# Threshold attention on one core: GpSimd made to wait for two-operand DVE steps, and a new order of all steps

## The chip, the cores and the metric

The kernel runs on one core of one Trainium2 chip. The metric is the device time of one execution in microseconds (us). The kernel before took 198.44 us (median of 3 runs, 197.9 to 199.52).

## The reference

Inputs are Q, K and V with 8 batches, 12 heads, 512 positions and 64 dimensions in float32, and a threshold of 0.1.

```
scores  = einsum('bhqd,bhkd->bhqk', Q, K) / sqrt(64)
weights = exp(scores - max(scores))
weights = weights / (sum(weights) + 1e-10)
weights = where(weights > 0.1, weights, 0)
weights = weights / (sum(weights) + 1e-10)
out     = einsum('bhqk,bhkd->bhqd', weights, V)
```

A row of weights has 512 entries with sum 1. With these inputs hardly any weight passes 0.1, so nearly every row of the output is zero.

## The kernel before, in words

The kernel writes zeros to the whole output and then computes only the few rows in which some weight may pass the threshold. There are 96 heads, taken as 48 pairs (two heads, one on each half of the partitions) and as 24 quads (two pairs, one load of K and Q).

**First part, all rows, in 16 bits.** For each quad SP (SyncE) issues the loads of K (L357) and Q (L361). TensorE transposes K (L392), ACT or DVE copies it from PSUM as float32 (L400, L402), GpSimd casts it to float16 (L411). GpSimd casts Q to float16 (L382), TensorE transposes it (L421), DVE copies it from PSUM (L427). For each pair there are four score steps (`sc`, L449, two matmuls each). Each score matmul fills one PSUM bank, and one exponent step (`ex`) empties it: on ACT with its exponential (L458) or on DVE with an integer approximation (L460). There are 384 exponent steps. The sum step (`sm`, L479, four matmuls) adds the exponents and a sharpened copy of them into a sum bank in PSUM, which collects a group of pairs. The groups have 24, 22 and 2 pairs (the last with L495). There is one sum bank.

**End of a group.** When all its sums are in, `y` (L521 on ACT), `d` (L532), `fl` (L537) and `mx` (L541) on DVE find the rows that may hold a large weight; `d` reads the sum bank for the last time, after which the next group's sums may begin.

**Second part, the rows found, in float32.** A group is followed by stages of up to 8 pairs (7 stages in all: three for group 0, three for group 1, one for group 2). A stage x runs `m` (L550, DVE), `ix` (L556, PE), `qi` (L561, DVE: the row numbers), `gq` (L567, GpSimd: an indirect DMA gathers the rows of Q), `xm` (L575 or L578, PE), `xev` (L585 or L587), `xqk` (L600 or L594, PE: scores against the float32 K that was kept), `xexp` (L606, ACT), `xcut` (L610), `xkeep` (L614), `oi` (L625) and `vi` (L619) on DVE, `gv` (L629, GpSimd: gathers rows of V) and `scatter` (L641, GpSimd: writes them to the output).

**Norms, a check on the 16-bit part.** For each quad `bits` squares the float16 Q and K: on GpSimd as two products (L436), on ACT (L438), or on DVE as a shift (L440). `norms` (L510, PE, four matmuls) adds the squares, and `nm` (L528, DVE) takes their maximum. For quads 0 to 7 the norms lie in spare rows of the sum banks of groups 0 and 1, and `nm` reads those banks at the end of the group; for quads 8 to 23 they have a PSUM bank of their own at the end. The checks (L789 to L804) end in one matmul (L813) and a branch: if a check fails, a slow exact loop runs.

**Order.** All steps of all engines stand in one table, `ORDER` (L13): a word is a step's number and its engine. Each engine runs its steps in that order, and an instruction waits only for the data and buffers that it needs. DVE and GpSimd stand in no fixed order to each other, except through such data. Buffers come from pools: 7 PSUM banks called `one`, 32 large SBUF buffers called `big` (loads, transposed K, float16 pairs, squares). `warm` steps (L367) run matmuls on zeros at the start, `spare` steps (L371, 20 of two matmuls each) run idle matmuls near the end; in the table of before they stand between the last norms.

Of the kernel before, what the change touches and what calls it, by code (L numbers as in the profile page):

```python
# [94 lines left out]
def kernel(  # L95
# [130 lines left out]
    is_norm = consts.tile([P, len(NORMS)], f32)  # L226
# [177 lines left out]
    def do_kh(eng, q, n):  # L404
        dst, src = qk_b[big("qk", q)][:, 1, n, :], kt_b[big("kt", q)][:, n, :]
        if eng == "ACT":
            nc.scalar.copy(dst, src)
        elif eng == "DVE":
            nc.vector.tensor_copy(dst, src)
        else:  # L410
            nc.gpsimd.tensor_copy(dst, src)  # L411
# [483 lines left out]
```

## Time and profile before

| what | value |
|---|---|
| runs | 199.52, 197.9, 198.44 us (median 198.44) |
| profiled execution | 198.32 us, its span 196.1 us, mean granted TensorE clock 0.945 |
| PE busy | 171.2 us (87%) |
| DVE busy | 164.8 us (84%), 369 instructions |
| ACT busy | 147.0 us (75%), 294 instructions |
| GpSimd (POOL) busy | 139.2 us (71%), 212 instructions |
| data moved | 38.28 MB, 195 GB/s over the span |

The span is from the first to the last instruction; the time of an execution holds 2.2 us more. A busy share is a mean over stages with different limits. A DVE instruction that has started and is held up counts as busy, so DVE's share contains such waits. A granted clock of 1.00 is 2.4 GHz and of 0.50 is 1.2 GHz; a value between is a mean over a stretch that holds both.

### The profile page before, as it was taken

Reading aid. Unit: us, or ns where it says so; the run is one execution under the profiler, and the core shown is the slowest. Engines: PE = TensorE matmul, PEld = TensorE weight load, DVE = VectorE, ACT = ScalarE, POOL = GpSimd, SP = SyncE. Lnnn points to the kernel's source line nnn. Section 1 sums busy time; section 2 is a strip of 40 time slices with the busy share of each in tenths; the row PEclk is TensorE's granted clock in tenths of the full one; section 3 lists DMA queues with packets and bytes.
Section 4 is the critical chain, followed back from the end, with each engine's and each line's share of the span. In section 5 each row is a group of like instructions: output and inputs, shape, how many; then the busy total and the mean of one; then the engine's idle time right before and its main releaser. Section 6 shows DMA issues by size and latency. Waiting matters only on the chain. (4 is left out here: it accounts for less than half of the span.)

```text
span 196.1 us, 6072 instructions
## 1 busy us (share of the span) xinstructions
PE 171.2 (87%) x2312; PEld 71.5 (36%) x2312; DVE 164.8 (84%) x369; ACT 147.0 (75%) x294; POOL 139.2 (71%) x212
## 2 busy tenths in 40 slices
PE   5799999999999997799799799999298396999960
PEld 2344343443443342243342343334032134643540
DVE  7769999999999997789999999999969957579320
ACT  0879999999999997989799699989169129483100
POOL 5459889999795999089999984969729441515570
PEclk9999999999999999999999999999859667599998
DMA  6998998998998979799879853699990000000000
GB/s 152 280 256 194 276 259 228 292 217 199 282 230 272 295 240 313 270 333 241 315 209 323 220 160 76 133 283 410 415 388 15 0 5 1 5 3 3 6 6 4
DMA packets 67550, 38.28 MB, mean 195 GB/s; under 512 B 52035, under 2 KB 64446, under 8 KB 67520
## 3 DMA queue, kind: packets, MB, share of 16 engines
q1 hardware_dynamic: 64464, 36.97, 67.5%
q10 hardware_dynamic: 2384, 0.79, 1.7%
q8 instruction: 18, 0.29, 0.6%
q0 software_dynamic: 672, 0.13, 0.5%
q14 instruction: 12, 0.10, 0.2%
HBM read 25.58 MB, written 12.79 MB: 196 GB/s over the span
## 5 line engine op out<-in xcount | busy, mean ns | idle before, releaser
L458 ACT ACTIVATE e<-one 128x512 f16<-128x512 f32 x228 | 118.6, 629 | 17.9 <-PE one L449 15.3
L460 DVE TENSOR_SCALAR e<-one 128x512 uint16<-128x512 f32 x156 | 99.5, 681 | 4.6 <-PE one L449 2.9
L449 PE MATMUL one<-big 64*128 64x512 f16 x384 | 71.9, 401 | 10.9 <-DVE e L460 7.3
L436 POOL TENSOR_TENSOR big<-big 128x512 bf16<-128x512 f16 x56 | 57.7, 1055 | 4.6 <-PE one L392 4.6
L479 PE MATMUL sum<-e,w_s 128*32 128x512 f16 x736 | 57.9, 403 | 0.4 <-DVE y L532 0.4
L411 POOL CAST big<-big 128x512 f16<-128x512 f32 x47 | 28.6, 624 | 9.6 <-ACT big L400 4.2
L449 PEld LDWEIGHTS <-big 64*128 64x128 f16 x384 | 18.9, 97 | 44.6 <-issue 37.9
L382 POOL CAST qh<-big 128x512 f16<-128x512 f32 x47 | 28.4, 619 | 8.7 <-DMA big<-in_Q_dram 7.1
L479 PEld LDWEIGHTS <-w_s 128*32 128x32 f16 x736 | 14.6, 98 | 31.9 <-issue 25.8
L400 ACT COPY big<-one 128x512 f32<-128x512 f32 (+1 forms) x38 | 20.9, 580 | 4.2 <-PE one L392 2.2
L427 DVE COPY big<-one 128x512 f16<-128x512 f16 (+1 forms) x52 | 19.6, 396 | 4.9 <-PE one L421 3.4
L392 PE MATMUL one<-identity_f,big 64*128 64x64 f32 x384 | 18.5, 236 | 2.8 <-DMA big<-in_K_dram 1.3
L392 PEld LDWEIGHTS one<-identity_f,big 64*128 64x128 f32 x384 | 16.8, 148 | 8.3 <-issue 1.8
L567 POOL DMA_INDIRECT qs<-in_Q_dram,idx x7 | 7.3, 1047 | 16.3 <-DVE idx L561 15.0
L629 POOL DMA_INDIRECT vr<-in_V_dram,idx x7 | 7.2, 1022 | 8.3 <-DVE idx L619 5.7
L440 DVE TENSOR_SCALAR big<-big 128x512 int32<-128x512 int32 x16 | 12.9, 838 | 0.1
L421 PEld LDWEIGHTS <-qh 64*128 64x128 f16 x384 | 8.9, 99 | 10.4 <-issue 5.0
L421 PE MATMUL one<-identity_h,qh 64*128 64x64 f16 x384 | 11.0, 197 | 1.8 <-POOL qh L382 1.0
L600 PE MATMUL one<-big,xq 128*32 128x512 f32 x92 | 10.9, 596 | 0.0
L402 DVE COPY big<-one 128x512 f32<-128x512 f32 (+1 forms) x14 | 9.0, 645 | 1.9 <-PE one L392 1.3
L641 POOL DMA_INDIRECT out_dram<-vr,idx x7 | 7.0, 1006 | 3.4 <-issue 3.3
L606 ACT ACTIVATE one<-one 128x512 f32<-128x512 f32 (+2 forms) x7 | 4.1, 579 | 6.7 <-PE one L600 4.2
(100 smaller groups left out, 108.1 us busy)
## 6 DMA issues: line engine op xcount, KB each, us to landing
out_dram<-zero SPq DMA_DIRECT2D x24, 512.0 KB, 6.8
big<-in_K_dram SPq DMA_DIRECT2D x92, 128.0 KB, 4.7
big<-in_Q_dram SPq DMA_DIRECT2D x22, 512.0 KB, 4.8
big<-in_Q_dram SPq DMA_DIRECT2D x3, 256.0 KB
big<-in_K_dram ACTq DMA_DIRECT2D x4, 128.0 KB, 4.8
big<-in_Q_dram ACTq DMA_DIRECT2D x1, 256.0 KB
qs<-in_Q_dram,idx POOLq DMA_INDIRECT x7
vr<-in_V_dram,idx POOLq DMA_INDIRECT x7, 2.3
```

The source lines that it names most:

```text
L382: nc.gpsimd.tensor_copy(dst, src)
L392: nc.tensor.matmul(dst[i][:, c:c + D], lhsT=src[ps, n0 + n, r, :], rhs=identity_f32[ps, ps], is_transpose=True, start=True, stop=True)
L400: nc.scalar.copy(dst, src)
L411: nc.gpsimd.tensor_copy(dst, src)
L421: nc.tensor.matmul(dst[i][:, c:c + D], lhsT=src[ps, n0 + n, r, :], rhs=identity_h[ps, ps], is_transpose=True, start=True, stop=True)
L427: nc.vector.tensor_copy(qk_b[big("qk", q)][:, 0, n0:n0 + k, i * SO * D:(i + 1) * SO * D], src)
L436: nc.gpsimd.tensor_tensor(out=dst[:, n, :], in0=src[:, n, :], in1=src[:, n, :], op=ALU.mult)
L440: nc.vector.tensor_scalar(dst.rearrange("p n c -> p (n c)").bitcast(i32), src.rearrange("p n c -> p (n c)").bitcast(i32), 2, 0x1FFF1FFF, o ...
L449: nc.tensor.matmul(one[at("one", ("sc", hp, t, h))][:], lhsT=qk[ps, 1, n, t * P:(t + 1) * P], rhs=qk[ps, 0, n, :], start=True, stop=True)
L458: nc.scalar.activation(dst, src, ACTF.Exp, scale=scale, bias=-11.0 * math.log(2.0))
L460: nc.vector.tensor_scalar(dst.bitcast(u16), src, scale * LOG2E * 1024.0, 4096.0, op0=ALU.mult, op1=ALU.add)
L479: nc.tensor.matmul(dst[32 * j:32 * j + 32, :], lhsT=w, rhs=x, start=first, stop=False, skip_group_check=True)
```

## The change

GpSimd's casts and products get a wait. Each DVE step that reads two SBUF operands, or copies or shifts from SBUF to SBUF (`qcast`, `kh`, `bits`, `fl`, `m`), is noted by `alone`; the next cast or product of GpSimd in the table waits until that DVE step has ended (`behind`). GpSimd's indirect DMAs get no such wait. `oi` no longer reads two SBUF tensors: a new DVE step `qf` writes a float copy of the output index, and `oi` takes it as a scalar operand. The norms of quads 0 to 7 leave the sum banks and get a `one` bank for themselves, as those of quads 8 to 23 have; `nm` runs twice, not three times, and no longer stands between a group's sums and the release of the sum bank. `warm` has 8 steps, not 5. `ORDER` is another table.

```
-    WARM = 5
+    WARM = 8
+    last_pair = [None]
+    def alone(inst):
+        last_pair[0] = inst
+        return inst
+    def behind(inst):
+        if last_pair[0] is not None:
+            tc.add_manual_dep(inst.ins, last_pair[0].ins.name,
+                              mybir.DependencyInfo(mybir.DependencyClass.Sync, mybir.DependencyReason.DATA),
+                              reason="one engine at a time on the shared port")
+            last_pair[0] = None
+        return inst
 ...
-            nc.gpsimd.tensor_copy(dst, src)
+            behind(nc.gpsimd.tensor_copy(dst, src))
 ...
-                nc.gpsimd.tensor_tensor(out=dst[:, n, :], in0=src[:, n, :], in1=src[:, n, :], op=ALU.mult)
+                behind(nc.gpsimd.tensor_tensor(out=dst[:, n, :], in0=src[:, n, :], in1=src[:, n, :], op=ALU.mult))
 ...
-        if q < LATE:
-            g = norm_of[q]
-            assert g in begun
-            dst, i, first = sum_b[at("sum", g)], norm_of[:q].count(g), False
-        else:
-            dst, i, first = one[at("one", "late")], q - LATE, "late" not in begun
+        part = int(q >= LATE)
+        dst, i = one[at("one", ("norms", part))], q - PARTS[part][0]
 ...
-        nc.vector.scalar_tensor_tensor(out=idx_b[at("ix", x)][0:n, 0:2],
-                                       in0=one[at("one", ("ix", x))][0:n, 0:1].to_broadcast([n, 2]), scalar=-1.0,
-                                       in1=base[0:n, 0:2, x], op0=ALU.mult, op1=ALU.add)
+        nc.vector.tensor_scalar(idx_b[at("ix", x)][0:n, 0:1], one[at("one", ("ix", x))][0:n, 0:1], -1.0,
+                                base[0:n, 0, x:x + 1], op0=ALU.mult, op1=ALU.add)
+    def do_qf(eng, x):
+        nc.vector.tensor_scalar(ix_b[at("ix", x)][0:n, :], one[at("one", ("ix", x))][0:n, 0:1], -1.0,
+                                base[0:n, 1, x:x + 1], op0=ALU.mult, op1=ALU.add)
 ...
-        nc.vector.scalar_tensor_tensor(out=to, in0=accs[0:n, x:x + 1], scalar=-(FAR - S), in1=to, op0=ALU.max, op1=ALU.add)
+        nc.vector.tensor_scalar(idx_b[at("ix", x)][0:n, 2:3], accs[0:n, x:x + 1], -(FAR - S), ix_b[at("ix", x)][0:n, :],
+                                op0=ALU.max, op1=ALU.add)
```

Counted in the two tables: exponents on ACT 228, then 232; on DVE 156, then 152. `bits` on GpSimd 28 in both, on DVE 16, then 12, on ACT 4, then 8. Copies of K from PSUM on ACT 38, then 36, on DVE 14, then 16. `y` of groups 1 and 2 on ACT, then of group 1 on DVE and of group 2 on ACT. In the new table all of norms 0 to 7 stand together at the end of group 0, 16 norms stand together behind the last `xqk`, and the 20 `spare` steps stand last of all, behind the checks.

## Rows read from the trace of the kernel before

**Rows 1.** Busy time by stretch: PE, PEld, DVE, ACT, POOL, granted clock, DMA share, GB/s
```profile
8.00:14.00 6.00, 5.52 (x54) 2.24 (x51) 4.25 (x11) 4.52 (x11) 3.96 (x12) 1.00 1.21 249
...
20.00:138.00 118.00, 112.70 (x1647) 45.00 (x1640) 112.00 (x207) 110.78 (x223) 100.83 (x156) 1.00 0.93 255
138.00:147.00 9.00, 5.32 (x59) 2.03 (x58) 7.11 (x9) 3.01 (x7) 4.40 (x6) 0.63 1.00 404
...
151.40:160.60 9.20, 5.58 (x54) 1.88 (x56) 7.78 (x11) 2.51 (x5) 3.77 (x5) 0.64 0.01 2
160.60:171.00 10.40, 8.84 (x110) 5.00 (x106) 6.40 (x16) 6.54 (x13) 4.04 (x4) 0.66 0.02 4
```

**Rows 2.** Timeline of DVE: start, duration, line, tiles, count
```profile
91.55 1.70 DVE L440 TENSOR_SCALAR big<-big 128x512 int32<-128x512 int32 x2
...
108.10 1.96 DVE L625 SCALAR_TENSOR_TENSOR idx<-accs,idx 128x1 int32<-128x1 f32 x1
...
136.23 4.86 DVE L625 SCALAR_TENSOR_TENSOR idx<-accs,idx 128x1 int32<-128x1 f32 x1
...
149.12 5.26 DVE L440 TENSOR_SCALAR big<-big 128x512 int32<-128x512 int32 x1
```

**Rows 3.** Timeline of POOL in the same stretch, with its idle time in brackets
```profile
139.04 2.03 POOL L436 TENSOR_TENSOR big<-big 128x512 bf16<-128x512 f16 x2
145.67 2.04 POOL L436 TENSOR_TENSOR big<-big 128x512 bf16<-128x512 f16 x2 [4.60 <-PE one L392]
...
152.07 2.02 POOL L436 TENSOR_TENSOR big<-big 128x512 bf16<-128x512 f16 x2
```

**Rows 4.** Timeline of PE: its first matmul after the stall
```profile
141.74 1.63 PE L449 MATMUL one<-big 64*128 64x512 f16 x5 [3.66 <-DVE e L460]
```

**Rows 5.** One line's instructions: duration in ns, least, median and longest
```profile
L625 DVE SCALAR_TENSOR_TENSOR idx<-accs,idx x7: 157/198/4862, 108.1 to 184.8; 128x1 int32<-128x1 f32 x5, 96x1 int32<-96x1 f32 x1, 64x1 int32<-64x1 f32 x1
...
L440 DVE TENSOR_SCALAR big<-big x16: 408/424/5259, 18.9 to 177.5; 128x512 int32<-128x512 int32 x16
```

**Rows 6.** Exponents on ACT (L458) by stretch: busy time, clock, DMA
```profile
20.00:138.00 118.00, 94.89 (x184) 1.00 0.93 255
138.00:161.00 23.00, 8.40 (x17) 0.70 0.41 163
```

**Rows 7.** Exponents on DVE (L460) by stretch
```profile
20.00:138.00 118.00, 80.17 (x126) 1.00 0.93 255
138.00:161.00 23.00, 9.29 (x15) 0.70 0.41 163
```

**Rows 8.** Groups by line and shape: count, busy us, mean ns, idle before
```profile
L458 ACT ACTIVATE e<-one 128x512 f16<-128x512 f32 x228 | 118.6, 629 | 17.9 <-PE one L449 15.3 <-PE one L510 1.6 <-issue 0.4
L460 DVE TENSOR_SCALAR e<-one 128x512 uint16<-128x512 f32 x156 | 99.5, 681 | 4.6 <-PE one L449 2.9 <-PE one L510 1.3
...
L600 PE MATMUL one<-big,xq 128*32 128x512 f32 x92 | 10.9, 596 | 0.0
...
L438 ACT ACTIVATE big<-big 128x1024 bf16<-128x1024 f16 x4 | 4.3, 1072 | 0.0
...
L619 DVE TENSOR_SCALAR idx<-accs,base 128x1 int32<-128x1 f32 x5 | 1.0, 204 | 0.0
```

**Rows 9.** Timeline of all engines from the end of group 1 to the end
```profile
161.14 0.69 DVE L528 TENSOR_REDUCE nmax<-sum 128x1 f32<-128x512 f32 x1 [1.62 <-PE sum L479]
...
166.22 1.02 POOL L567 DMA_INDIRECT qs<-in_Q_dram,idx  x1 [4.36 <-DVE idx L561]
...
180.76 0.62 PE L510 MATMUL one<-big,w_n 128*32 128x512 bf16 x8
...
187.25 2.05 PE L371 MATMUL one<-identity_f 128*128 128x128 f32 x16
...
190.44 0.09 PEld L813 LDWEIGHTS one<-identity_f,okm 128*1 128x1 f32 x2 [1.33 <-DVE nmax L528]
```

**Rows 10.** DMA issues: KB each, median us from issue to landing
```profile
big<-in_Q_dram SPq DMA_DIRECT2D x22, 512.0 KB, 4.8
```

More of the change, by code (lines that the diff above doesn't have):

```diff
@@ L131 @@
     LATE = 8
-    NORMS = (4, 4)
-    norm_of = [g for g, k in enumerate(NORMS) for _ in range(k)]
-    assert sum(NORMS) == LATE and all(GROUPS[g] + 2 * k <= 32 for g, k in enumerate(NORMS)) and 2 * (NQ - LATE) <= 32
+    PARTS = (range(0, LATE), range(LATE, NQ))
+    assert all(2 * len(k) <= 32 for k in PARTS)
     J = 8
@@ L408, in do_kh @@
         elif eng == "DVE":
[L409 removed]
+            alone(nc.vector.tensor_copy(dst, src))
         else:
[L411 removed]
+            behind(nc.gpsimd.tensor_copy(dst, src))
     def do_qtr(eng, u):
@@ L730 @@
             gives=[("big", ("qk", q))])
[L731 to L734 removed]
+        part = int(q >= LATE)
+        head = PARTS[part][0]
+        after = [("norms", head)] if q > head else [("sc", NP - 3, 0)] if part else []
+        add(("norms", q), {"PE": 0.22}, 0.23, [("bits", q, 1)] + after, 8 * q + (9 if q < LATE else 60),
+            lambda e, q=q: do_norms(e, q), takes=[("one", ("norms", part))] if q == head else [], gives=[("big", ("v", q))], mode="c")
         add(("z", q), {"SP": 0.6}, 0.1, [("sc", 2 * q, 0), ("const", 0)], 8 * q - 6, lambda e, q=q: do_zero(e, q))
@@ L740 @@
             gives=[("one", "spare")] if j == SPARE - 1 else [], mode="c")
-    add(("nm", "late"), {"DVE": 0.6}, 0.12, [("norms", q) for q in range(LATE, NQ)], 9999, lambda e: do_nm(e, "late"),
-        gives=[("one", "late")])
+    for part, qs in enumerate(PARTS):
+        add(("nm", part), {"DVE": 0.6}, 0.12, [("norms", q) for q in qs], 9999 if part else 8 * LATE + 20,
+            lambda e, part=part: do_nm(e, part), gives=[("one", ("norms", part))])
     for g in range(NG):
@@ L751 @@
         sums = [("sm", hp, t) for hp in pairs for t in range(SO)]
-        norms = [("norms", q) for q in range(LATE) if norm_of[q] == g]
         step("y", {"DVE": 0.6, "ACT": 0.5}, 0.12, sums, do_y, takes=[("y", g)])
         step("d", {"DVE": 0.64}, 0.12, ["y"], do_d)
-        if norms:
-            step("nm", {"DVE": 0.6}, 0.12, sums + norms, do_nm, pr=pr + 3)
-        add(("sumdone", g), {"NONE": 0.0}, 0.0, [("d", g)] + ([("nm", g)] if norms else []), 0, lambda e: None,
-            gives=[("sum", g)])
+        add(("sumdone", g), {"NONE": 0.0}, 0.0, [("d", g)], 0, lambda e: None, gives=[("sum", g)])
         step("fl", {"DVE": 0.7}, 0.12, ["d", ("const", 1)], do_fl)
@@ L804, in do_check_end @@
         nc.vector.tensor_reduce(okm[:], oks[:], axis=AX.X, op=ALU.min)
-    add(("check", 0), {"DVE": 0.15}, 0.2, [("nm", "late")] + [("nm", g) for g in range(NG) if ("nm", g) in plan.ids], 999, do_check_norm)
+    add(("check", 0), {"DVE": 0.15}, 0.2, [("nm", part) for part in range(len(PARTS))], 999, do_check_norm)
     add(("check", 1), {"DVE": 0.15}, 0.2, [("fl", g) for g in range(NG)], 999, do_check_count)
```

63 lines of the change are left out of this document (27 added, 36 removed).

## The prediction

> **What bounds the kernel now.** I read the busy time by stretch first. From 20 to 138 us PE, DVE and ACT are each busy 110 to 113 of 118 us at clock 1.00: nothing but more engines or less work would help there much. From 138 to 171 us the picture is another one: in 138 to 147 and in 151.4 to 160.6 us PE is busy 5.3 and 5.6 of 9 us, ACT 3.0 and 2.5, and the granted clock is 0.63 and 0.64, a mean of full and half; 160.6 to 171 has 0.66 [rows 1]. So what to look for is what begins at 138 and at 151.
>
> The timeline of DVE answers it. A step `oi` (L625) starts at 136.23 and takes 4.86 us, and a `bits` (L440) starts at 149.12 and takes 5.26 [rows 2]; the median of these lines is 0.20 and 0.42 us [rows 5]. Both read and write SBUF only. Beside them GpSimd runs one instruction after the other, and they end when GpSimd runs dry: its products of 139.04 end at 141.07 and it then idles 4.60 us, DVE's step ends at 141.09; its products of 152.07 end at 154.09, DVE's step at 154.38 [rows 2, 3]. While DVE stands, the exponents behind it are late, the PSUM banks stay full, and PE idles 3.66 us until DVE's first exponent after the stall [rows 4]; then it comes back at the lower clock, as the stretch's mean of 0.63 says [rows 1]. So the stall is 4.7 us, and the damage is larger.
>
> By the Trainium skill, page "SBUF — State Buffer", section "SBUF: two separate sides", DVE and GpSimd share a port pair as an exclusive lock: whoever starts first holds it for its instruction. The trace agrees that one engine blocks the other, but not with the length: by that rule DVE would wait for one product, about 1 us, and the two stalls would be worth some 2 us, not 9.5. What the rows show is that DVE did not get its turn between one GpSimd instruction and the next. The rule makes a rival of its own (B).
>
> **The change, part by part.** The sum goes from the profiled execution, 198.32 us, with a span of 196.1 and 2.2 us around it; it lies 0.12 under the median of the runs.
>
> *The waits, and `oi` without a second SBUF operand.* Exponent steps measure progress. From 20 to 138 us ACT did 94.89/118.6 x 228 = 182 and DVE 80.17/99.5 x 156 = 126, so 308 in 118 us or 2.61 per us [rows 6 to 8]. From 138 to 161 us they did 8.40/118.6 x 228 + 9.29/99.5 x 156 = 16 + 15 = 31, which at 2.61 per us is 11.8 us of work; it took 23.1 us up to 161.1, where the sums of group 1 are complete and `nm` (L528) starts [rows 6, 7, 9]. **Gain 11.3 us**, between 9.5 (the two stalls alone) and 13. In the table of before, the GpSimd steps that ran during both stalls stand behind the DVE step that they held up (but for one pair of products at the second), so the waits would hold back just these; and the new `oi` has the form of `vi` (L619), which takes 0.20 us [rows 8]. Smaller hold-ups between 91 and 110 us (two `bits` in 1.70 instead of 0.84, an `oi` in 1.96 instead of 0.20 [rows 2, 5]) make 2.6 us of DVE; as ACT shares the exponents I count half, **1.3 us** (0 to 2.6).
>
> What the waits add: before group 1 ends, the new table has only four DVE `bits`, one `fl` and three `m` of this kind, hence at most six waits on GpSimd (a wait notes only the last such step). Behind a waiting cast stand the casts of the next quads, and behind those the transposes and scores. GpSimd is busy 100.8 of 118 us [rows 1], so some waits show. No row has such a wait; the nearest bounds are 0 (DVE done already) and the length of an exponent in front of the DVE step, 0.64 us, times six, 3.8. I take 0.8, near the lower end, since DVE is mostly the one that is behind.
>
> *Norms in own banks.* `nm`, 0.69 us, stands in front of `d` and with it of the next group's sums [rows 9]. At the end of group 0 this gives **0.7 us**; that of group 1 is in the tail below. In exchange norms 0 to 7 are done only at the end of group 0, so that up to eight of the 32 large buffers hold squares until then. Counting in the tables how many exponents lie between the release of a buffer and the use of the load that goes into it: Q of quads 11, 13, 14, 15 and 16 have 18, 20, 22, 13 and 17, where the old table has 23 and more for these. 13 exponents are 13/2.61 = 5.0 us, a Q load lands 4.8 us after its issue [rows 10]. That is just enough; I take **0.7 us** for late loads and with the GpSimd waits **+1.5 us** in all (0 to 5).
>
> *Start.* Three more `warm` steps and another order. In 8 to 14 us ACT idles 1.5 us and DVE 1.75 [rows 1]; that bounds the gain. I take **0.8 us** (0 to 1.5). `qf`, seven small DVE steps of 0.15 to 0.2 us, lies in stages where DVE waits for the gathers; it would cost 1.4 us at most, and is in the bounds of the waits.
>
> *The tail,* from the end of group 1 (call it T0, 161.1 before, so 35.0 us to the end of the span). Of the new order at full clock:
> - `gq` of stage 3 came at 166.22, 5.1 us after T0 [rows 9]; without `nm` 4.4.
> - The 16 exponents of group 2: ACT has 12, 0.52 us each (118.6/228), and one square of 1.07 [rows 8]: 7.3 us, with a score in front and a sum behind T0 + 8.5.
> - `xqk` of stages 3, 5, 4: 16, 12 and 16 matmuls of 0.118 us (10.9/92 [rows 8]), 5.2 us; with the transposes, copies and the short stage 6 between and behind them I estimate T0 + 16.6.
> - 16 norms: two in 0.62 us, 0.22 for each more [rows 9], 3.4 us; but three squares on ACT stand behind the last `xexp`, 3 x 1.07, so the last norms end near T0 + 21.6.
> - The 20 `spare` steps now stand in PE's queue in front of L813: 40 matmuls at 2.05/16 = 0.128 us [rows 9], 5.1 us, T0 + 26.7. `nm` and the checks run beside them in some 1.3 us, so this order throws 3.8 us away.
> - From L813 to the end of the span 196.1 - 190.44 = 5.7 us [rows 9]: T0 + 32.4. GpSimd's 14 indirect DMAs from `gq` of stage 3 on, about 1.3 us each with the gap, end near T0 + 24 and are covered by PE; without the spares they would be next.
> So the tail gives **2.6 us**.
>
> The sum: 198.3 - 11.3 - 1.3 - 0.7 - 0.8 - 2.6 + 1.5 = 183.1, **183 us**. With all terms at their good ends it is about 178, at their bad ends about 190.
>
> **The rivals.**
>
> *A. One fall of the clock more.* The new table lets GpSimd's four products of quads 20 and 21 stand in front of `fl` of group 1, without a wait between: if GpSimd is behind by then, DVE is held once more at the worst place, and PE, which has no spare steps there any longer, stands. For it: 160.6 to 171 us has 0.66 already now, after such a group's end [rows 1]. Against it: from 20 to 138 us, with group 0's end inside, the clock stays 1.00. Price: half of what the two stalls cost, 11.3/2 = 5.6: 189 us.
>
> *B. The stall is not the operands.* If DVE is held for one instruction at most, as the page's rule says, then the long stalls have another cause and the waits remove nothing of them. Left are the start, the norms and the tail: 198.3 - 0.8 - 0.7 - 2.6 + 1.5 = 196 us. Against it: both stalls end within 0.3 us of GpSimd's last product.
>
> *C. Loads become the bound, slower than before.* Place: the five Q loads named above, around the end of group 0. For it: the DMA share is 0.93 already in 20 to 138 us [rows 1], and the new table leaves them 5 to 8 us. If they land in 9 to 10 us instead of 4.8, each stops GpSimd's cast and the scores behind it by some 4.3 us: 183 - 0.7 + 5 x 4.3 = 204 us. It decides from 3.2 us for each of the five (16 us in all). Against it: the bytes are the same.
>
> *D. The same time:* half of C, or A twice with long waits on GpSimd, 196.5 to 200.4.
>
> **How the numbers follow.** The forecast has 0.60, A 0.20, B 0.04, D 0.06, C 0.10. The likeliest is 183 us. The range that holds 8 in 10 takes the forecast with its bounds and most of A: 178 to 193. Faster by over 1% (about what can be told from no change) is the forecast, A and B: 0.84; within 1% D: 0.06; slower C: 0.10.
>
> **What would show it right or wrong.** Right: the longest L440 below 1.5 us and `oi` near 0.2; no stretch between 20 us and group 1's end with PE idle over 2 us; group 1's sums complete near 147 us; clock 1.00 from there on; 20 spares in one block of about 5 us in front of the last matmul. Wrong: a DVE step on SBUF of several us beside GpSimd's products; GpSimd idle in front of casts, with DVE as releaser, for more than 4 us in all; casts of Q that wait for DMA around the end of group 0; a tail of over 36 us, or one at clock 0.50.

## The result and the profile after

The changed kernel takes 183.03 us (median of 4 runs, 182.27 to 187.93), the kernel before 198.5 us beside it: ratio 0.920, 95% interval 0.915 to 0.926. The profiled execution took 183.06 us, with a span of 181.1 us at a mean clock of 0.971 (before 0.945). The forecast was 183; but two parts of its sum were off by 6 us in opposite directions, as the profile shows. Here and below a median is over all runs of a kernel, while a ratio and its interval are of the undisturbed runs alone, of which the kernel before has too few on the fourth chip for a ratio.

Busy time by stretch, the changed kernel (PE, PEld, DVE, ACT, POOL, granted clock, DMA share, GB/s), for [rows 1]:

```profile
8.00:14.00 6.00, 5.71 (x74) 2.79 (x72) 4.08 (x11) 5.19 (x12) 2.26 (x4) 1.00 0.98 259
20.00:138.00 118.00, 116.40 (x1723) 47.50 (x1722) 112.90 (x221) 114.37 (x232) 103.89 (x153) 1.00 0.90 263
138.00:147.00 9.00, 6.25 (x116) 2.50 (x110) 6.51 (x13) 6.83 (x15) 5.21 (x6) 0.98 0.66 256
147.00:151.00 4.00, 3.60 (x59) 2.40 (x58) 3.08 (x9) 3.49 (x7) 1.04 (x1) 0.50 0.01 2
151.00:160.00 9.00, 6.08 (x82) 2.58 (x80) 3.83 (x15) 2.27 (x6) 4.69 (x5) 0.86 0.03 5
160.00:171.00 11.00, 9.87 (x90) 3.54 (x88) 7.20 (x32) 7.86 (x13) 5.93 (x6) 0.84 0.03 5
```

From 20 to 138 us PE is now busy 116.4 of 118 us instead of 112.7, at full clock. From 147 to 151 us there is a clock of 0.50 again. DVE's two lines of [rows 5] (ns, least, median, longest), under their new line numbers `bits` L454 and `oi` L635:

```profile
L454 DVE TENSOR_SCALAR big<-big x12: 406/417/559, 74.2 to 169.6; 128x512 int32<-128x512 int32 x12
...
L635 DVE TENSOR_SCALAR idx<-accs,ix x7: 200/205/214, 97.9 to 169.0; 128x1 int32<-128x1 f32 x5, 96x1 int32<-96x1 f32 x1, 64x1 int32<-64x1 f32 x1
```

The longest are 0.56 and 0.21 us, where they were 5.26 and 4.86. The exponents by shape, for [rows 8] (count, busy us, mean ns, idle before):

```profile
L472 ACT ACTIVATE e<-one 128x512 f16<-128x512 f32 x232 | 120.1, 653 | 6.1 <-PE one L463 5.7
L474 DVE TENSOR_SCALAR e<-one 128x512 uint16<-128x512 f32 x152 | 96.8, 683 | 3.3 <-PE one L463 2.4 <-issue 0.2
```

And from 20 to 138 us, on ACT and then on DVE, for [rows 6, 7]:

```profile
20.00:138.00 118.00, 99.39 (x193) 1.00 0.90 263
...
20.00:138.00 118.00, 84.45 (x134) 1.00 0.90 263
```

That is 99.39/120.1 x 232 = 192 and 84.45/96.8 x 152 = 133, so 325 exponents or 2.75 per us, against 308 and 2.61 before. The difference is not spread evenly. By the same working from shorter stretches, 20 to 78 us has one exponent more than before, 112 to 138 has four, and 78 to 112, the stretch behind the end of group 0 where its stages run, has twelve. The busy times of that stretch, before and then changed:

```profile
78.00:112.00 34.00, 30.13 (x422) 11.68 (x414) 31.50 (x59) 29.48 (x59) 28.06 (x36) 1.00 0.91 273
...
78.00:112.00 34.00, 32.57 (x466) 13.47 (x458) 31.02 (x69) 31.91 (x66) 29.32 (x40) 1.00 0.94 268
```

The end of group 1 and the end of the kernel, for [rows 9] (start, duration, engine, line, idle before):

```profile
140.94 1.48 PE L493 MATMUL sum<-e,w_s 128*32 128x512 f16 x24
142.35 0.82 PE L463 MATMUL one<-big 64*128 64x512 f16 x6
144.45 0.68 DVE L532 TENSOR_SCALAR y<-sum 64x512 f32<-64x512 f32 x1 [1.96 <-PE one L463]
144.55 2.56 ACT L472 ACTIVATE e<-one 128x512 f16<-128x512 f32 x5 [2.17 <-PE one L463]
145.92 0.63 PE L509 MATMUL sum<-e,w_s 128*32 128x128 f16 x32 [2.75 <-DVE y L539]
...
171.52 0.43 PE L519 MATMUL one<-big,w_n 128*32 128x512 bf16 x4
171.88 4.93 PE L369 MATMUL one<-identity_f 128*128 128x128 f32 x40
174.97 0.69 DVE L535 TENSOR_REDUCE nmax<-one 128x1 f32<-128x512 f32 x1 [4.17 <-remote]
...
176.74 0.38 PE L822 MATMUL one<-identity_f,okm 128*1 128x128 f32 x2
```

By PE's records, whose ends are modelled, group 1's sums are complete at 142.4 us (161.1 before) and its scores end at 143.17. DVE and ACT start only at 144.45 and 144.55: for 1.3 us nothing runs on any of the three. I call it the standstill. What DVE and ACT waited for is PE's signal: both rows name PE's scores (L463) as what released them, and the trace has the semaphore updates of the last sums and of these scores only from 144.43 to 144.61 us, 2.0 us behind the end that the sums' record gives. It happens again at the end: the last norms (L519) end at 171.95 by their record, and `nm`, which reads them, starts at 174.97 (its releaser is too long past to be named; on the fourth chip, in experiment 7, it is PE's L519). There PE itself was not held up, as its 40 spare products follow in 4.93 us and DVE reads the result of its last matmul at 177.16; the signal alone was late. The clock falls behind the standstill. From 142.4 to the span's end it is 38.7 us, where I had 32.4. The 20 spares stand as one block of 4.93 us in front of the last matmul.

GpSimd's waits for DVE's `bits`, and for loads of Q (total us, times, longest):

```profile
POOL big L450 <- DVE big L454: 5.0, 3, 3.8
...
POOL qh L396 <- DMA big<-in_Q_dram: 0.7, 1, 0.7
```

### The profile page after: what moved, and what is told of

Its sections match the earlier page's. It is cut to its first block, busy times and chain, and to the rows that moved or that the text cites. A ratio compares the mean times of both kernels' runs of the same rounds, so it can differ in the third digit from the quotient of the medians.

```text
span 181.1 us, 6122 instructions
## 1 busy us (share of the span) xinstructions
PE 165.5 (91%) x2324; PEld 71.2 (39%) x2324; DVE 150.3 (83%) x369; ACT 149.7 (83%) x298; POOL 138.5 (76%) x211
## 4 chain that ended last, share of the span: by engine, by line
PE 79%; DMA 7%; DVE 5%; POOL 3%; ACT 2%; issue 1%; another core or an unknown queue 1%; SPq 0%; DVEq 0%; POOLq 0%; ACTq 0%
PE one L463 27%; PE sum L493 23%; PE one L406 7%; PE one L611 6%; PE one L435 4%; DMA big<-in_Q_dram 4%; DMA qs<-in_Q_dram,idx 3%; PE one L369 3%; PE one L519 2%; PE one L586 2%; PE sum L509 2%; POOL big L450 1%; PE one L563 1%; POOL big L425 1%
## 5 line engine op out<-in xcount | busy, mean ns | idle before, releaser
L472 ACT ACTIVATE e<-one 128x512 f16<-128x512 f32 x232 | 120.1, 653 | 6.1 <-PE one L463 5.7
L474 DVE TENSOR_SCALAR e<-one 128x512 uint16<-128x512 f32 x152 | 96.8, 683 | 3.3 <-PE one L463 2.4
L463 PE MATMUL one<-big 64*128 64x512 f16 x384 | 66.0, 390 | 1.1 <-DVE big L441 1.0
L450 POOL TENSOR_TENSOR big<-big 128x512 bf16<-128x512 f16 x56 | 56.8, 1037 | 5.0 <-DVE big L454 5.0
L493 PE MATMUL sum<-e,w_s 128*32 128x512 f16 x736 | 55.5, 384 | 0.0
L463 PEld LDWEIGHTS <-big 64*128 64x128 f16 x384 | 18.5, 96 | 37.5 <-issue 28.9
L396 POOL CAST qh<-big 128x512 f16<-128x512 f32 x46 | 27.3, 612 | 4.3 <-PE one L463 2.2
L414 ACT COPY big<-one 128x512 f32<-128x512 f32 (+1 forms) x36 | 20.2, 602 | 1.4 <-PE one L406 1.3
L611 PE MATMUL one<-big,xq 128*32 128x512 f32 x92 | 13.0, 670 | 1.2 <-issue 1.1
L416 DVE COPY big<-one 128x512 f32<-128x512 f32 (+1 forms) x16 | 10.1, 635 | 0.8 <-PE one L435 0.7
L452 ACT ACTIVATE big<-big 128x1024 bf16<-128x1024 f16 x8 | 8.3, 1060 | 0.0
```

Source lines behind the costliest of these rows:

```text
L396: behind(nc.gpsimd.tensor_copy(dst, src))
L450: behind(nc.gpsimd.tensor_tensor(out=dst[:, n, :], in0=src[:, n, :], in1=src[:, n, :], op=ALU.mult))
L463: nc.tensor.matmul(one[at("one", ("sc", hp, t, h))][:], lhsT=qk[ps, 1, n, t * P:(t + 1) * P], rhs=qk[ps, 0, n, :], start=True, stop=True)
L472: nc.scalar.activation(dst, src, ACTF.Exp, scale=scale, bias=-11.0 * math.log(2.0))
L474: nc.vector.tensor_scalar(dst.bitcast(u16), src, scale * LOG2E * 1024.0, 4096.0, op0=ALU.mult, op1=ALU.add)
L493: nc.tensor.matmul(dst[32 * j:32 * j + 32, :], lhsT=w, rhs=x, start=first, stop=False, skip_group_check=True)
```

## The experiments

The attention kernels ran on three chips, called second to fourth here, and the last small kernel of experiment 8 on one more; whether the chip of the result is one of them is not on record. The kernels of one set ran beside each other; medians in us:

| chip | before | changed | others |
|---|---|---|---|
| of the result | 198.5 | 183.0 | |
| second | 200.1 | not run | old order with waits 186.9, no waits 186.1, old `oi` 176.8, no spares 173.8 |
| third | 198.9 | 185.6 | half the zero stores 184.6, fillers in the tail 185.2 |
| fourth | 200.6 | 177.7 | no spares 173.1 |

**1. The waits and the new `oi` on the old order.** Kernel before with `alone`, `behind`, `qf` and the new `oi`; its order, norms and spares stay.

```diff
-            nc.gpsimd.tensor_copy(dst, src)
+            behind(nc.gpsimd.tensor_copy(dst, src))
...
-        nc.vector.scalar_tensor_tensor(out=to, in0=accs[0:n, x:x + 1], scalar=-(FAR - S), in1=to, op0=ALU.max, op1=ALU.add)
+        nc.vector.tensor_scalar(to, accs[0:n, x:x + 1], -(FAR - S), ix_b[at("ix", x)][0:n, :], op0=ALU.max, op1=ALU.add)
```

> The kernel before with its own order, norms and warm steps; only the waits on GpSimd and the new form of oi are added (qi and qf as two DVE steps one behind the other). Theory P (what is gained comes from DVE getting its turn beside GpSimd): no L441 or L455 of this kernel over 1.5 us, the two stalls of 4.9 and 5.3 us gone, group 1's sums complete near 150 us instead of 161, 186 to 189 us in all. Rival O (the new order and the norms' own banks bring most of it): both DVE steps shorter, but GpSimd's waits or the old order keep the gain under 4 us: 195 to 198 us.

Measured 186.93 (184.66 to 188.53), ratio 0.930 (0.920 to 0.940). The `bits` in this kernel, in ns:

```profile
L455 DVE TENSOR_SCALAR big<-big x16: 411/426/3721, 19.0 to 170.6; 128x512 int32<-128x512 int32 x16
```

And its busy times in the loop, with the columns of [rows 1]:

```profile
20.00:138.00 118.00, 109.54 (x1595) 43.78 (x1594) 108.22 (x205) 106.07 (x214) 95.80 (x150) 0.99 0.87 238
```

One hold of 3.72 us is left: the GpSimd steps beside it stand ahead of the DVE step in the old order, so no wait covers it. So theory P held but for this hold, and group 1's sums were complete near 154.5 us, not 150. 13.2 us of the gain come without the new order; but PE's 109.5 of 118 us (in an execution of 188.53 us, the longest of the four) show that the loop itself is not the changed kernel's.

**2. The new order without the waits.** The changed kernel with this:

```diff
     def behind(inst):
-        if last_pair[0] is not None:
-            tc.add_manual_dep(...)
         return inst
```

> The changed kernel without the waits: casts and products of GpSimd never wait for a DVE step for the port's sake; order, norms, warm steps and the new oi stay. P: among the DVE bits, fl and m there are holds as before, some of 2 to 5 us; only 4 bits, one fl and three m stand ahead of group 1's end, so less is at stake than before: 185 to 191 us. O: the order does without the waits, no such step over 1.5 us, 182 to 184 us.

Measured 186.08 (184.58 to 187.96), ratio 0.922 (0.912 to 0.933). Timeline of all engines in this kernel around its longest hold:

```profile
75.66 4.57 DVE L454 TENSOR_SCALAR big<-big 128x512 int32<-128x512 int32 x1
...
76.70 2.04 POOL L450 TENSOR_TENSOR big<-big 128x512 bf16<-128x512 f16 x2
78.68 0.67 POOL L336 MEMSET qs<- 128x64 f32 x7
79.28 0.67 POOL L336 MEMSET vr<- 128x64 f32 x7
79.89 0.80 POOL L396 CAST qh<-big 128x512 f16<-128x512 f32 x1
...
80.88 0.58 PE L463 MATMUL one<-big 64*128 64x512 f16 x1 [2.38 <-DVE e L474]
```

The hold is back, over casts, products and 14 memsets, 4.57 us for a step of 0.42, and PE idles 2.38 us until DVE's next exponent. A step `m` was held as well, for 3.87 us. So the waits take the holds away; the order does not. Yet the order, with the norms' own banks, the `warm` steps and the new `oi`, brought 14.0 us without them, as much as the waits and the new `oi` did on the old order. Both together, with the old form of `oi` (next), gave 23.3 us on this chip. So with the new order in place the waits are worth 9.2 us (186.1 to 176.8), and with the waits in place the rest of the change 10.1 us (186.9 to 176.8); in neither pair do the runs overlap.

**3. The old form of `oi` with waits and new order.**

```diff
-        nc.vector.tensor_scalar(idx_b..., accs..., -(FAR - S), ix_b..., op0=ALU.max, op1=ALU.add)
+        nc.vector.scalar_tensor_tensor(out=idx_b..., in0=accs..., scalar=-(FAR - S), in1=ix_b..., op0=ALU.max, op1=ALU.add)
```

> The changed kernel with oi again as an operation of two SBUF operands (the float copy as second operand instead of a scalar); the waits do not know of it. P: of its seven steps the three of group 0's stages meet GpSimd at work and are held, at least one for 1.5 us or more: 184 to 189 us. O: all near 0.2 us, 183 us.

Measured 176.84 (173.61 to 179.88), ratio 0.868 (0.858 to 0.878). Its `oi`, in ns:

```profile
L635 DVE SCALAR_TENSOR_TENSOR idx<-accs,ix x7: 144/158/886, 101.6 to 164.7; 128x1 int32<-128x1 f32 x5, 96x1 int32<-96x1 f32 x1, 64x1 int32<-64x1 f32 x1
```

One of seven was held, for 0.7 us, less than theory P's 1.5. What the new form of `oi` is worth in time is not shown, as the changed kernel did not run on this chip. An estimate: the kernel without spares took 173.8 us here and the spares cost some 4 us on the fourth chip (experiments 4 and 7), which puts the changed kernel near 178 us, not below this one. That the time lay far below 183 asked for the changed kernel itself as a control.

**4. Without the spares.** First on the second chip:

```diff
     def do_spare(eng):
+        return
```

> The changed kernel without its 20 spare steps. By the prediction's term for the tail they delay the last matmul by 5.1 us less the 1.3 us of nm and checks: 179 us. Rival: the last scatter, issued at 173.9 us in the profile, and its landing hold the end, so that only 1 to 2 us come back: 181 to 182 us.

Measured 173.8 (171.41 to 176.53), ratio 0.864 (0.854 to 0.874), below both expectations; without the changed kernel on this chip it does not tell what the spares cost. Then the control, on the third chip, with two kernels meant to explain the standstill:

> The changed kernel once more, unaltered, as the control for the other kernels: the version without the 20 spare products was measured beside the kernel before alone. Theory T (the 2 us in which three engines stood idle at the end of group 1, and the clock's falls behind it, belong to one execution and not to the order of the work): the spread of its times reaches well below 183, the profile shows less than 1 us idle between the last exponents of group 1 and y_1, and the ratio to the kernel before comes to 0.87 to 0.90. Rival U (the order makes that idle time each time): 2 us idle there again, clock at half after it, ratio 0.92. Either way the spares stand as one block of 4.9 us before the last matmul.

Measured 185.58 (182.57 to 188.43), ratio 0.930 (0.915 to 0.946): theory U's standstill was there again, 2.00 us in front of `y_1`, with clock 0.50 from 150 to 160 us.

**5. Half of the zero stores left out.**

```diff
     def do_zero(eng, q):
+        if q >= 12:
+            return
```

> The changed kernel without the zero stores of the last 12 of the 24 pairs of head pairs; that half of the output stays unwritten but for the scattered rows. Theory Z (the stores that fill the DMA engines up to 144 us hold something that the engines wait for at the end of group 1): the DMA engines are quiet after some 110 us, no idle of 2 us of ACT, DVE and PE before y_1, and 2 to 5 us less than the changed kernel as it is on this chip. Rival N (the stores cost nothing there): within 1 us of it.

Measured 184.64 (183.78 to 187.52), within 1 us of the control. Timeline of this kernel:

```profile
144.06 0.82 PE L463 MATMUL one<-big 64*128 64x512 f16 x6
146.20 0.68 DVE L532 TENSOR_SCALAR y<-sum 64x512 f32<-64x512 f32 x1 [1.99 <-PE one L463]
146.29 5.06 ACT L472 ACTIVATE e<-one 128x512 f16<-128x512 f32 x10 [2.19 <-PE one L463]
```

And its busy times ahead of that:

```profile
138.00:142.00 4.00, 4.00 (x66) 1.38 (x64) 3.75 (x8) 3.89 (x9) 3.84 (x5) 1.00 0.00 0
```

The DMA engines are idle and the wait for PE's signal is the same 2 us. The stores are not its cause.

**6. Fillers in the tail instead of spares at the end.**

```diff
+    def fill(dst, k):
+        for j in range(k):
+            nc.tensor.matmul(dst, lhsT=identity_f32[:], rhs=identity_f32[:], start=True, stop=True)
...
     def do_spare(eng):
+        return
...
     def do_xm(eng, x):
+        if x == 3:
+            fill(one[at("one", ("xm", x))][:, 0:P], 6)
```

> The changed kernel with the 20 spare products taken from the end and 14 of the same products put where TensorE waits in the tail: 6 ahead of the first gathered stage of group 1, 4 ahead of its first score product, 4 ahead of the last group's row index (each writes a bank that the next step overwrites). If the clock's fall in the tail is what is left to win: no stretch of the tail at clock under 0.9 and 3 to 6 us less than the control (5 of the spares at the end, less some 1 to 2 us of fillers that are not covered). Rival: the fillers delay the chain by as much as the clock gives (0.25 us each at full clock, 3.5 us in all): 1 to 2 us less than the control.

Measured 185.23 (183.97 to 186.2) beside the control's 185.58: nothing gained. Timeline of PE in this kernel:

```profile
153.01 2.93 PE L370 MATMUL one<-identity_f 128*128 128x128 f32 x12
```

And the stretch with its clock:

```profile
150.00:155.00 5.00, 5.00 (x79) 4.16 (x79) 3.04 (x9) 1.50 (x2) 3.22 (x4) 0.50 0.04 9
```

The clock was at half when the fillers came, since the standstill lies ahead of them. There six of them (two passes each) take 2.93 us: `xm` starts behind them at 155.87 us, where in the control it starts at 152.85 without a gap before it. At the end `nm` starts at 176.33 us, 1.9 us behind the last norms (174.38), and with no spares beside it this late signal delays the last matmul. So the spares' gain is given back.

**7. Changed kernel and no spares, side by side.** On the fourth chip:

> The changed kernel, unaltered, beside the version without spares on one chip. In three profiles it stood still for 1.3 us on all of TensorE, VectorE and ScalarE behind the last score products of group 1, and its clock fell to half behind that; the version without spares and the one with the old form of the output index, profiled on another chip, did not. Theory C (the chip or the execution makes that stillness): same and no-spares versions agree here, both with it or both without it; 183 to 186 with it, 177 to 180 without it. Rival L (the program as it lies in memory makes it): this one has it, with 183 to 186, whatever chip it is, and the version without spares has not.

Measured 177.66 (176.45 to 179.65), all six runs below every run of the same kernel on the third chip. Timeline of the same kernel here:

```profile
141.34 0.82 PE L463 MATMUL one<-big 64*128 64x512 f16 x6
141.52 0.69 DVE L532 TENSOR_SCALAR y<-sum 64x512 f32<-64x512 f32 x1
141.83 3.04 ACT L472 ACTIVATE e<-one 128x512 f16<-128x512 f32 x6 [0.45 <-PE one L463]
...
165.49 4.73 PE L369 MATMUL one<-identity_f 128*128 128x128 f32 x40
165.60 0.69 DVE L535 TENSOR_REDUCE nmax<-one 128x1 f32<-128x512 f32 x1 [1.10 <-PE one L519]
...
170.15 0.38 PE L822 MATMUL one<-identity_f,okm 128*1 128x128 f32 x2
```

The same program has no standstill here: `y_1` starts 0.1 us behind the sums, and `nm` 0.04 us behind the norms, which end at 165.56. Theory C held: the standstill belongs to the chip or the execution, not to the program. The other profiles of this order agree: none on the second chip and neither on the fourth has it, all three on the third have. A fetch of instructions, an obvious suspect, is not seen to cause it: on the chip of the result one is recorded in 144.0 to 144.5 us, when most of the standstill is over, and here, without a standstill, one in 142 to 143 us.

> The changed kernel without its 20 spare products ahead of the last matmul. Theory C: 3.8 to 5 us less than the changed kernel on the same chip, the spares' 4.9 us less the clock that the last product loses; the stillness behind group 1 as in the changed kernel here. Rival L: 9 to 11 us less, with no stillness and the clock full through the first half of the tail.

Measured 173.14 (172.15 to 174.5), some 4 us below the changed kernel (4.5 by the medians, 4.3 by the fastest runs), without overlap of the runs; it is the fastest version tried. Its end:

```profile
164.40 0.17 DVE L814 TENSOR_REDUCE okm<-oks 128x1 f32<-128x12 f32 x1
164.62 0.38 PE L823 MATMUL one<-identity_f,okm 128*1 128x128 f32 x2 [1.19 <-DVE okm L814]
165.85 0.94 POOL L653 DMA_INDIRECT out_dram<-vr,idx  x1 [0.30 <-DVE over_i L827]
```

The last matmul follows on `okm`, not on spares, and GpSimd's last scatter is what ends last now.

**8. The hold by itself.** Three kernels with nothing but chains on GpSimd and steps on VectorE, started together by ACT. Their core, with the sections that the text speaks of:

```
prod: gpsimd.tensor_tensor(v, qk, qk, mult)        128x512 f16 -> bf16
bits: vector.tensor_scalar(w2, w, 2, 0x1FFF1FFF)   128x512 int32, SBUF to SBUF
section([prod] * 6,  [ps, ps, bits, ps])           # ps: copy out of PSUM
section([prod] * 12, [ps, ps, bits, ps])
section([prod] * 6,  [ps, ps, oi_two, ps])
section([prod] * 6,  [ps, ps, oi_one, ps])
```

> A kernel of its own, which computes none of the reference: sections that an ACT copy starts together on GpSimd (6 or 12 f16 products of 128x512 of 1.04 us, or 6 or 12 casts of 0.61 us, back to back) and on VectorE (two PSUM copies, then the integer shift of two SBUF operands, or the one-column step in its two forms, then a PSUM copy). If VectorE's held step gets in between two GpSimd instructions: it lasts up to 1 us beyond its 0.4 us, as long behind 12 products as behind 6. If it is held until GpSimd has nothing ready: it lasts to the end of the chain, 4 to 5 us behind 6 products and some 10 us behind 12, half of that behind casts, and 1 us or less where each product waits for a paced ACT step. The one-column step in the form with a pointer operand 0.2 us throughout, in the form with two tensor operands as long as the shift.

DVE's steps in it: alone, behind 6 products, behind 12, then `oi` with two tensor operands and with a pointer operand, both behind 6:

```profile
5.75 0.42 DVE L64 TENSOR_SCALAR w<-w 128x512 int32<-128x512 int32 x1
...
16.73 1.15 DVE L64 TENSOR_SCALAR w<-w 128x512 int32<-128x512 int32 x1
...
23.72 1.15 DVE L64 TENSOR_SCALAR w<-w 128x512 int32<-128x512 int32 x1
...
50.50 0.89 DVE L67 SCALAR_TENSOR_TENSOR o<-c 128x1 int32<-128x1 f32 x1
...
57.43 0.20 DVE L70 TENSOR_SCALAR o<-c 128x1 int32<-128x1 f32 x1
```

The hold is 0.73 us whether 6 or 12 products stand there, so it is one instruction; and the step with a pointer operand (one column as scalar, 0.20 us alone too) is not held. A hold of one instruction is the rule of the Trainium skill ("SBUF — State Buffer", section "SBUF: two separate sides"), and these rows agree with it. The attention kernel shows both: in the kernel before, two `bits` took 1.70 us together amid six products back to back [rows 2], so each waited for one instruction at most, while other steps were held over four and more. GpSimd beside these two `bits`:

```profile
90.74 6.63 POOL L436 TENSOR_TENSOR big<-big 128x512 bf16<-128x512 f16 x6
```

Two further kernels looked for the difference:

```diff
-prod: gpsimd.tensor_tensor(v, qk, qk, mult)
+prod(i): gpsimd.tensor_tensor(vs[i], qk, qk, mult)          # second and third: a tile for each
...
-section([prod] * 6,  [ps, ps, bits, ps])
+section([conv, qc, prod, prod] * 2, [ps, ps(n), bits, ps])  # third: n = 64 to 448, five sets
```

> A kernel of its own, which computes none of the reference: VectorE's integer shift or one-column step starts amid a chain of GpSimd instructions. In the first such kernel the products all wrote one tile, took 1.10 us each, and VectorE's step got in after the one that ran (0.42 us became 1.15). Here every GpSimd instruction writes its own tile, so that none follows on another's result, as in the attention kernel, where a product took 1.02 us and VectorE was held over four to six of them. Theory G (GpSimd gives the port back only where it pauses between two instructions): with tiles of their own the step lasts until the chain ends, some 4 to 5 us behind 6 products and 10 behind 12; with one tile, or with a wait for an ACT step that has long been met ahead of each product, 1.15 us again. Rival O (one instruction at a time whatever follows): 1.15 us or less everywhere, and the 4 to 5 us of the kernel before need another cause. Rival K (casts count too): the chain of casts alone holds the step in this form; it did not where they wrote one tile.

Two of its steps, behind 6 products with tiles of their own and in a chain of casts and products:

```profile
12.26 1.03 DVE L68 TENSOR_SCALAR w<-w 128x512 int32<-128x512 int32 x1
...
84.12 1.15 DVE L68 TENSOR_SCALAR w<-w 128x512 int32<-128x512 int32 x1
```

Theory G fell: 1.15 us at most in all sections.

> A kernel of its own, which computes none of the reference. GpSimd runs two casts, two products, two casts and two products back to back, 6.4 us with the tiles apart, as in the stretch of the kernel before in which VectorE was held for 4.86 us; VectorE's integer shift (first half) or one-column step (second half) starts at seven moments 0.07 us apart within the first of them. Five sets of these: with nothing beside them, with ScalarE exponents, with TensorE products, with loads of 512 KB from DRAM, with all three. The first two kernels of this kind gave the step its turn behind one instruction, 1.15 us at most. Theory M (whether VectorE gets its turn at the boundary of two GpSimd instructions depends on the moment): some of the seven last 2 us or more with nothing beside them. Theory W (the other engines' or the DMA's work on the same memory makes VectorE miss its turn): 1.2 us at most with nothing beside, 2 us and more with the loads, the exponents or all. Rival O: 1.2 us at most everywhere, and the kernel's long holds stay without a cause.

The longest with nothing beside, and the same moment with loads beside at a DMA share of 1.11:

```profile
39.37 1.28 DVE L72 TENSOR_SCALAR w<-w 128x512 int32<-128x512 int32 x1
...
182.16 1.28 DVE L72 TENSOR_SCALAR w<-w 128x512 int32<-128x512 int32 x1
```

Also 1.28 with exponents and with products beside. M and W fell for each of these alone; in the set with all three at once the step came after GpSimd's chain had ended, so that case was not tried. Rival O stands: with nothing else going on DVE is held for one instruction. Why it is held over four and more at some places of the attention kernel stays open.

## Why the prediction was right, and where it was not

The signs named beforehand. Right: `bits` below 1.5 us (0.56 at most) and `oi` near 0.2 (0.21), the spares as one block of 5 us (4.93), no PE idle over 2 us between 20 us and the end of group 1 (1.0 at most; the 2.75 us come behind it). Not right: group 1's sums near 147 us (142.4). The clock at 1.00 behind group 1 and a tail below 36 us: not on the chip of the result (0.50 from 147 to 151 us, 38.7 us), but nearly so on the fourth (from 141.4 to 174.5, 33.1 us, with 0.66 in 150 to 155 us). Of the signs of being wrong one came: GpSimd's waits for `bits` make 5.0 us, more than the 4 named, though in front of products and not of casts; they did no harm that shows (below).

*That the two stalls were holds by GpSimd:* right in the place. For `bits` it is shown by experiment 2, where holds of several us return with the waits gone; for the 4.86 us of `oi` it is argued from the rows alone, since no run brought that hold back. Rival B's sum, 196, was wrong; its rule is right for the hold alone and for some places of the kernel, not for the long holds.

*The size and the owner of the gain up to T0: the step that failed.* My terms put T0 at 161.1 - 11.3 - 1.3 - 0.7 - 0.8 + 1.5 = 148.5 (the text's "near 147" did not even fit them); it was 142.4 and 141.4. The term "smaller hold-ups, 1.3" is the one that was too small, and with it the opening sentence that little was to be had from 20 to 138 us: I took the loop's 2.61 exponents per us as fixed and gave the new order almost nothing for it. It is 2.75: over 118 us 325 - 308 = 17 exponents, 17/2.61 = 6.5 us, where the terms for this stretch (1.3 and 0.7 gained, 1.5 lost) come to 0.5. Twelve of the 17 lie in 78 to 112 us, the stretch of those hold-ups. Experiments 1 and 2 show that neither waits nor order alone have it (PE busy 109.5 of 118 us in both, sums complete near 154.5 us in the first and `y_1` at 154.3 in the second); on that same chip, with both and the old `oi`, PE is busy 114.4 of 118 us and `y_1` at 146.3. I priced the order only through its load distances, as a cost. How the gain of the loop divides between fewer holds and the better order is not shown. The start, 0.8, was about right: by 20 us there are 2.6 exponents more than before, 1.0 us. Late loads and waits, +1.5: about 0, Q casts wait 0.7 us for DMA, and the longest wait on DVE, 3.8 us up to 121.8, costs PE nothing: it is busy all of 118 to 122 us and all of 120 to 125.

*The tail, 32.4 us:* right in its own working where PE's signals come in time: 33.1 on the fourth chip. Without the spares and with the clock at 1.00 the norms end there 21.3 us behind the sums (142.16 to 163.43), where the working had 21.6. With the spares the sum is hit by two errors that cancel in part: the clock of 0.66 puts the norms' end 24.2 us behind the sums, and from the last matmul to the end it takes 4.3 us instead of 5.7. On the chip of the result the standstill (2.0 us from the sums to `y_1` instead of 0.1) and the clock behind it make 38.7; how much each has is not measured. It is not rival A: `fl` took 0.69 us, DVE was not held, and PE stood for another reason. A had the place and the consequence, not the cause.

*The spares, 3.8 us thrown away:* some 4 measured (4.6 us lie between the norms' end and the last matmul on the fourth chip, 1.2 without them). That GpSimd's scatters would be next is seen too.

So 183 was hit by -6.1 in the loop against +6.3 in the tail, and that they cancel is luck: nothing in the prediction stands for late signals of PE. Without the standstill, on the fourth chip, the kernel takes 177.7, just below the lower end of the range.

## What to carry to other kernels

Where a short step of SBUF operands alone lasts microseconds, look at what GpSimd runs beside it; making GpSimd wait for that one step costs little when GpSimd has slack, and the form with a pointer operand was not held in the small kernels. A rate measured in a loop with hidden hold-ups is not the loop's rate: price an order by what each engine could do, not by the rate it had. Where several engines stand still for no visible reason, look for the semaphore that releases them, since the recorded end of a matmul is modelled. Count filler work at the end of a queue as path, and run the unchanged candidate as a control on each chip before comparing variants.

## What was not expected of the hardware

- One program has two times by chip: 176.5 to 179.7 us on one, 182.6 to 188.4 on another. In the profiles of the second, and of the chip of the result, PE's signal to DVE and ACT comes 2.0 us late behind group 1 and 1.4 to 3.5 us late behind the last norms, and the clock falls to half behind the first; in those of the other chips both come within 0.1 us. The program is excluded, and so are the zero stores; what delays the signals is open. The kernel before has no such two times: 198.5 and 198.9 us on the chip of the result and the third, 200.1 and 200.6 on the others.
- DVE held by GpSimd: one instruction in a kernel of these two engines (0.42 to 1.28 us), one at some places of the full kernel, and up to 5.3 us over casts, products and memsets at others. Open too.
